# One hybrid decoder layer on one core: full-row attention scores, priority for partial-sum copies and additions, and a shifted first softmax

## The chip, the cores and the metric

The kernel runs on one core of a Trainium2 chip. The metric is device time in microseconds (us). Its engines are named as in the profile: PE multiplies matrices (PEld loads its stationary operand), DVE, ACT and POOL work on vectors, SP starts most DMAs. PE's granted clock is given as a share of full speed: 1.00 is the 2.4 GHz level, 0.50 the 1.2 GHz level.

## The reference

One layer for 512 tokens of 1024 features, in float32. After an RMS norm one wide projection gives the inputs of two branches. Branch A is causal attention in a window of 128 tokens with 8 query heads and 2 key heads of 64 features, a relative-position bias from a table, and a learned sink per head that joins the softmax's maximum and denominator. Branch B is gated linear attention. Gates merge both; a SwiGLU feed-forward layer of 2816, a per-layer embedding gate and a final norm follow. What the change touches is this part:

```python
s = jnp.einsum('bnqhgd,bnkhd->bnhgqk', qb, kb) * (HEAD_DIM ** -0.5)
s = s + band_relative_bias(rel_table)
s = jnp.where(valid[None, :, None, None], s, -1e30)
m = jnp.maximum(jnp.max(s, axis=-1, keepdims=True), sink)
pr = jnp.exp(s - m)
denom = jnp.sum(pr, axis=-1, keepdims=True) + jnp.exp(sink - m)
o = jnp.einsum('bnhgqk,bnkhd->bnqhgd', pr / denom, vb)
```

## The kernel before

**Products.** Each float32 operand is split into a high part (a cast on ACT, L111) and a low part (a subtraction, L112, on DVE and in some cases on POOL). A product is then three matmuls, high by high, high by low and low by high (L121 to L123), added up in PSUM. Large projections go through a scheme of seven products in place of eight: `quad_pair` for one pair of output tiles, in four steps named for example qa0.0 to qa0.3. It keeps running sums in PSUM; between steps ACT copies an intermediate sum out of the bank in which PE continues (L542, L548, L554, L562; the tiles named u and v), and DVE adds (L534). The second step of a pair writes into the bank that the first copy reads, so PE waits for that copy. The sums of weight blocks that the scheme needs are made on POOL (L255); `Weights` loads, sums and splits the blocks a few units ahead of their use.

**Order.** Each engine works through a queue in a fixed order. A scheduler sets it from the order in which the program issues its instructions; work inside `tc.high_priority(offset=...)` is placed as though issued that much sooner. `drive(stream, other)` takes one step of a projection and then one step of another generator, so a `yield` decides beside which step a piece stands.

**Stages.** First come the norm and projection v0 with values and low-rank gates, then v2, then a small matmul that expands the bias table (bias_ps, from the copy rts), the attention keys (kaps), and v1, the rest of the linear branch's values (about 59 to 82 us). Then the attention queries qa0 and qa1 run (about 82 to 107 us), while the generator `log_decay` issues 16 scans (L705) that accumulate the linear branch's decay. Next are the linear branch's keys and queries, qk0 to qk3, and gates og0 and og1 (to about 226 us); `attention` is driven beside these.

**Attention.** There are 8 items, one for each block of 128 tokens and key head. Item j has the steps scores, transposes and values, and in between a softmax: bias added (L756), the maximum mx (L761), m with the sink (L764), its negative nm (L766), dl (L768), exponentials on ACT (L770, L773), de and rd (L775, L777) and scaling (L779). Transposes (L789) follow on PE. In items 0 and 1, the first block, scores are plain float32 matmuls of 64 rows (L750). In the others a score is two matmuls: L753 over 128 rows, in which the stationary tile holds the query's high and low parts in two halves and the moving tile the key's high part twice, and L754 over 64 rows, the query's high part by the key's low part. The low parts of the two key heads lie in one tile, kl, one in each half of its partitions.

Of the kernel before, what the change touches and what calls it, by code (L numbers as in the profile page):

```python
# [9 lines left out]
F32 = mybir.dt.float32  # L10
F32R = mybir.dt.float32r
# [22 lines left out]
def hybrid_layer(  # L34
# [427 lines left out]
                W.split_to(W.pos + u - 1)  # L462
        v0_evac(t, ps)

    hT.sums()


    bgk = cpool.tile([P, 4], F32, name="bgk")
    glag = cpool.tile([P, 2], F32, name="glag")
    sink = cpool.tile([P, 8], F32, name="sink")  # L470
    rt = cpool.tile([32, 8], F32, name="rt")
    oh = t2("oh")
    band = t2("band")
# [9 lines left out]
    nc.sync.dma_start(gple, norm_ple.rearrange("(k p o) -> p k o", p=P, o=1))  # L483
    nc.sync.dma_start(glag, gla_norm.rearrange("(j d) -> d j", d=P))
    nc.sync.dma_start(mraw, c_masks)
    nc.vector.tensor_scalar_mul(glag, glag, 0.5)
    masks = cpool.tile([P, 6, 32], U8, name="masks")
    nc.vector.tensor_copy(masks, mraw)


    def tok_inner(name, lhs, k0, nk, ncol, evac, per=2):
# [31 lines left out]
    def quad_pair(name, act, c, evac):  # L523

        pa, pb, pc = (bank(f"{name}p{x}") for x in "abc")
        H = (slice(0, 256), slice(256, 512))

        def product(ps, w, i, x, first=True):
            hi, lo = act.q(x)
            for k in range(4):  # L530
                mm3(ps, (w[0][:, i, k, :], w[1][:, i, k, :]), (hi[:, k, :], lo[:, k, :]), first and k == 0, k == 3, not first)

        def add(out, a, b):
            nc.vector.tensor_tensor(out=out, in0=a, in1=b, op=ALU.add)  # L534


        part = t2(f"{name}u"), t2(f"{name}v")
        p1, u2, u3, u4 = (part[i // 2][:, H[i % 2]] for i in range(4))
        run = pa[:, H[0]]
        w = W.take(f"{name}.0")  # L540
        product(run, w, 0, "b11")
        nc.scalar.copy(p1, run)  # L542
        product(pb[:, H[0]], w, 1, "b21")
        add(c[0][:, H[0]], pb[:, H[0]], p1)
        yield
        w = W.take(f"{name}.1")
        product(run, w, 1, "t2", False)
        nc.scalar.copy(u2, run)  # L548
        product(pc[:, H[0]], w, 0, "t1")
        add(u4, pc[:, H[0]], u2)  # L550
        yield
        w = W.take(f"{name}.2")
        product(run, w, 1, "t3", False)
        nc.scalar.copy(u3, run)  # L554
        product(pb[:, H[1]], w, 0, "b22")
        add(c[0][:, H[1]], pb[:, H[1]], u4)
        evac(0)
        add(c[1][:, H[1]], pc[:, H[0]], u3)
        yield
        w = W.take(f"{name}.3")  # L560
        product(run, w, 0, "t4", False)
        nc.scalar.copy(c[1][:, H[0]], run)  # L562
        evac(1)
        yield

# [51 lines left out]


    ps = bank("bias_ps")
    rts = t2("rts", (32, 16, 8))  # L620
    nc.vector.tensor_copy(rts, rt.unsqueeze(1).broadcast_to([32, 16, 8]))
    nc.tensor.matmul(ps[:, 0:NB], lhsT=rts.rearrange("b r h -> b (r h)"), rhs=oh[0:32, 0:NB], start=True, stop=True)
    bv = t2("bv")
    nc.vector.tensor_tensor(out=bv[:, 0:NB], in0=ps[:, 0:NB], in1=band[:, 0:NB], op=ALU.add)
# [10 lines left out]
    qa = a8("qa")  # L635


    qs = []
    k3 = a8("k3", (P, 3, 512), F32R)
    ks, kl = [k3[:, g, :] for g in range(2)], k3[:, 2, :]  # L640
    half = (slice(0, 64), slice(64, 128))

    def stack_k():
        for g in range(2):
            split((ks[g][half[g]], kl[half[g]]), k_aT[half[g]], eng=nc.gpsimd)
            nc.sync.dma_start(ks[g][half[1 - g]].bitcast(F32), ks[g][half[g]].bitcast(F32))

    def stack_q(i):
# [81 lines left out]
    def attention():  # L730
# [8 lines left out]
        def scores(j):  # L739
# [4 lines left out]
            for pair in range(2):  # L744
                ps = bank(f"sc{j}{pair}").rearrange("p (a b) -> p a b", a=2)
                keys = slice(kb * P, (n + 1) * P)
                for a in range(2):
                    h = 2 * pair + a
                    if n == 0:
                        nc.tensor.matmul(ps[:, a, :w], lhsT=qa[rows, h, tok(n)], rhs=k_aT[rows, 0:P], start=True, stop=True)  # L750
                        continue
                    q = qs[g][:, h, tok(n)]
                    nc.tensor.matmul(ps[:, a, :w], lhsT=q, rhs=ks[g][:, keys], start=True, stop=False)  # L753
                    nc.tensor.matmul(ps[:, a, :w], lhsT=q[rows], rhs=kl[rows, keys], start=False, stop=True)  # L754
                hs = slice(g * 4 + 2 * pair, g * 4 + 2 * pair + 2)
                nc.vector.scalar_tensor_tensor(  # L756
                    out=s[:, 2 * pair : 2 * pair + 2, :], in0=ps[:, :, :w], scalar=0.125, in1=bias[:, hs, 256 - w : 256],
                    op0=ALU.mult, op1=ALU.add,
                )
            mx = sm.tile([P, 4], F32, tag="mx", name=f"mx{j}")  # L760
            nc.vector.reduce_max(mx, s, axis=AX.X)  # L761
            m = sm.tile([P, 4], F32, tag="m", name=f"m{j}")
            sk = sink[:, 4 * g : 4 * g + 4]
            nc.vector.tensor_tensor(out=m, in0=mx, in1=sk, op=ALU.max)  # L764
            nm = sm.tile([P, 4], F32, tag="nm", name=f"nm{j}")
            nc.vector.tensor_scalar_mul(nm, m, -1.0)  # L766
            dl = sm.tile([P, 4], F32, tag="dl", name=f"dl{j}")
            nc.vector.tensor_tensor(out=dl, in0=sk, in1=m, op=ALU.subtract)  # L768
            es = sm.tile([P, 4], F32, tag="es", name=f"es{j}")
            nc.scalar.activation(es, dl, AF.Exp)  # L770
            su = sm.tile([P, 4], F32, tag="su", name=f"su{j}")
# [33 lines left out]
            if g:  # L805
                split(oaT.part(0, ALL, tok(n)), pov[n].rearrange("p (t q) -> p t q", t=4))

        yield
        for j in range(len(items) + 1):
            if j < len(items):  # L810
                scores(j)
                yield
            if j:
                transposes(j - 1)
                yield
                values(j - 1)
                if j != 2:
                    yield
# [559 lines left out]
```

## Time and profile before

| | us |
|---|---|
| median of 3 runs (lowest to highest) | 904.01 (902.99 to 907.49) |
| profiled execution, its own time | 906.57 |
| its span | 904.6 |
| PE busy (share of span) | 866.4 (96%) |
| DVE busy | 607.8 (67%) |
| ACT busy | 462.9 (51%) |
| POOL busy | 282.2 (31%) |

The mean granted clock of PE is 0.989. Shares of busy time are means over stages: PE is nearly always at work, so what remains is where it is not, where it runs at the lower clock, and how long its own instructions take. In the rows below a line such as L753 is a line of the kernel before; "idle before <-" names what ended an engine's idle time.

### The profile page before, as it was taken

What the parts mean: (1) busy time and instruction counts of PE and PEld (TensorE: products, weight loads), DVE (VectorE), ACT (ScalarE), POOL (GpSimd) and SP (SyncE); (2) the same over time, 40 slices, a digit from 0 to 9 for tenths busy, and PEclk for the clock granted to TensorE, in tenths of its full rate; (3) what the DMA queues carried; (4) which work ended last, traced back from release to release, by engine and by line L of the source; (5) the groups of instructions that cost most, each with busy time, mean ns of one, the idle gap of its engine ahead of it and who ended that gap; (6) DMA issues with size and microseconds to landing.
All of it is one profiled execution on the core that took longest, in us unless ns stands there. A gap on an engine that the chain in (4) does not pass through costs nothing.

```text
span 904.6 us, 15452 instructions
## 1 busy us (share of the span) xinstructions
PE 866.4 (96%) x6062; PEld 761.4 (84%) x6062; DVE 607.8 (67%) x874; ACT 462.9 (51%) x915; POOL 282.2 (31%) x229
## 2 busy tenths in 40 slices
PE   7889879999999999999999999999999999999996
PEld 5878777778977778888888899988999889998886
DVE  5768965666978753435459799734899536985564
ACT  5346665667766543423227655522566314554453
POOL 3673773333021110010033356022565034530001
PEclk9999979999999999999999999999999999999999
DMA  8364431124463444695213433432233422244502
GB/s 251 95 153 125 151 92 49 47 71 151 136 210 120 156 141 153 221 353 202 94 49 116 141 93 94 152 105 69 75 113 96 141 93 71 94 138 132 174 1 94
DMA packets 88235, 113.33 MB, mean 125 GB/s; under 512 B 6145, under 2 KB 64289, under 8 KB 87778
## 3 DMA queue, kind: packets, MB, share of 16 engines
q1 hardware_dynamic: 86706, 107.43, 37.5%
q0 software_dynamic: 1456, 4.92, 1.9%
q8 instruction: 47, 0.77, 0.4%
q14 instruction: 26, 0.21, 0.1%
HBM read 95.35 MB, written 15.93 MB: 123 GB/s over the span
## 4 chain that ended last, share of the span: by engine, by line
PE 79%; DVE 11%; issue 4%; ACT 3%; POOL 1%; DMA 1%; SPq 0%; POOLq 0%; ACTq 0%; DVEq 0%
DVE u L1257 2%; PE pov L801 1%; PE lv L892 1%; PE yaps L121 1%; PE sc L754 1%; PE yaps L123 1%; PE gt0ps L121 1%; PE gt0ps L123 1%; PE wo0ps L123 1%; PE wo0ps L121 1%; PE gt0ps L122 1%; PE yaps L122 1%; PE fo10ps L121 1%; PE fo10ps L122 1%; PE fo00ps L122 1%
## 5 line engine op out<-in xcount | busy, mean ns | idle before, releaser
L342 POOL TENSOR_TENSOR or<-om,mhalf 128x1 f32<-128x1 f32 x16 | 12.3, 770 | 63.8 <-DVE om L346 63.8
L111 ACT CAST act_h<-u 128x512 fp32r<-128x512 f32 x22 | 13.7, 622 | 27.2 <-DVE u L1257 27.2
L1257 DVE TENSOR_TENSOR u<-u,g 128x512 f32<-128x512 f32 x22 | 25.6, 1164 | 0.4
L884 DVE TENSOR_TENSOR zs<-zs,kq 128x512 f32<-128x512 f32 x28 | 19.8, 724 | 5.8 <-ACT zs L880 5.8
L342 POOL TENSOR_TENSOR h20r<-h20n,mhalf 128x1 f32<-128x1 f32 x1 | 0.6, 562 | 72.1 <-DVE h20n L351 72.1
L756 DVE SCALAR_TENSOR_TENSOR s_all<-sc,bias 128x512 f32<-128x512 f32 (+1 forms) x16 | 9.9, 622 | 11.6 <-PE sc L754 11.2
L976 ACT ACTIVATE own<-o,or 128x256 f32<-128x256 f32 x16 | 7.6, 475 | 18.6 <-POOL or L342 18.5
L878 DVE TENSOR_TENSOR zs<-G 128x512 f32<-128x512 f32 x24 | 15.8, 684 | 0.1
L773 ACT ACTIVATE s_all<-s_all,nm 128x256 f32<-128x256 f32 (+1 forms) x32 | 14.9, 469 | 1.5 <-DVE nm L766 1.5
L112 DVE TENSOR_TENSOR act_l<-u,act_h 128x512 fp32r<-128x512 f32 x22 | 14.9, 680 | 0.0
L801 PE MATMUL pov<-pT,kv 128*64 128x512 f32 x28 | 14.4, 612 | 0.4 <-ACT pT L791 0.4
L779 ACT ACTIVATE s_all<-s_all,rd 128x256 f32<-128x256 f32 (+1 forms) x32 | 12.8, 472 | 3.2 <-DVE rd L777 3.1
L1254 ACT ACTIVATE g<-g 128x512 f32<-128x512 f32 x22 | 13.9, 630 | 0.3
L121 PE MATMUL yaps<-qs,pa_h 128*128 128x512 f32 x32 | 13.6, 425 | 0.0
L879 ACT ACTIVATE zs<-zs 128x256 f32<-128x256 f32 x28 | 11.7, 419 | 3.5 <-DVE zs L878 3.0
L789 PE MATMUL pt<-ident,s_all 128*128 128x128 f32 x56 | 9.0, 285 | 4.5 <-ACT s_all L779 4.5
L1147 POOL DMA_DIRECT2D xr<-in_x x4 | 2.2, 566 | 34.9 <-PE gg3pb L123 34.9
L111 ACT CAST mx_h<-yg 128x512 fp32r<-128x512 f32 x8 | 5.0, 622 | 15.5 <-DVE yg L1092 15.5
L121 PE MATMUL gt0ps<-gt_h,xT_h 128*128 128x512 f32 x32 | 12.8, 401 | 0.0
L1243 POOL TENSOR_TENSOR r<-x10m,mhalf 128x1 f32<-128x1 f32 x1 | 0.6, 562 | 39.2 <-DVE x10m L351 39.2
L121 PE MATMUL wo0ps<-wo_h,mx_h 128*128 128x512 f32 x32 | 12.6, 395 | 0.0
L121 PE MATMUL wo1ps<-wo_h,mx_h 128*128 128x512 f32 x32 | 12.6, 395 | 0.0
(2782 smaller groups left out, 3839.6 us busy)
## 6 DMA issues: line engine op xcount, KB each, us to landing
mg<-mgd SPq DMA_DIRECT2D x8, 512.0 KB, 6.6
vd<-v_g SPq DMA_DIRECT2D x2, 1024.0 KB, 5.2
sild<-gw SPq DMA_DIRECT2D x8, 256.0 KB, 2.1
own<-vd SPq DMA_DIRECT2D x4, 512.0 KB, 5.2
own<-sild SPq DMA_DIRECT2D x4, 512.0 KB, 5.0
mgd<-gw SPq DMA_DIRECT2D x8, 256.0 KB, 2.6
ogd<-og SPq DMA_DIRECT2D x8, 256.0 KB, 3.5
mgd<-sgg SPq DMA_DIRECT2D x8, 256.0 KB, 4.5
```

The costliest lines, as they stand in the source:

```text
L111: nc.scalar.copy(hi, src)
L112: eng.tensor_tensor(out=lo, in0=src, in1=hi.bitcast(F32), op=ALU.subtract)
L121: nc.tensor.matmul(ps, lhsT=l[0], rhs=r[0], start=first, stop=False, **kw)
L122: nc.tensor.matmul(ps, lhsT=l[0], rhs=r[1], start=False, stop=False, **kw)
L123: nc.tensor.matmul(ps, lhsT=l[1], rhs=r[0], start=False, stop=last, **kw)
L342: return r, nc.gpsimd.tensor_tensor(out=r, in0=a, in1=mhalf, op=ALU.pow)
L773: nc.scalar.activation(s[:, a, :], s[:, a, :], AF.Exp, bias=nm[:, a : a + 1], accum_out=su[:, a : a + 1])
L801: nc.tensor.matmul(pov[n][rows, :], lhsT=v_a[:, kb + b, rows], rhs=pTs[j][b], start=(b == 0), stop=(b == nk - 1))
L878: pe.tensor_tensor(out=z3, in0=g3, in1=g3[:, :, b - 1 : b].broadcast_to([P, nb, 2 * b]), op=ALU.subtract)
L884: nc.vector.tensor_tensor(out=d4, in0=d4, in1=kq_, op=ALU.mult)
L1254: nc.scalar.activation(gs[e], gs[e], AF.Silu)
L1257: nc.vector.tensor_tensor(out=us[e], in0=us[e], in1=gs[e], op=ALU.mult)
```

## The change

Five edits are made:

- Copies and additions of `quad_pair` are issued with high priority (offset 1000). This holds for all its uses, in the feed-forward layer too.
- The low parts of the keys get a tile for each key head, kl[0] and kl[1], in which the other half's 64 partitions are set to zero by a POOL memset; the second score matmul goes over all 128 rows.
- The maximum is taken negated, with min against a negated sink `nsink`, so that the multiplication by -1 for each item is gone.
- In `attention` the first empty step is taken out and put in behind the second item's scores: scores 0 and 1 are issued one step sooner, and transposes 0 stand beside the same step as before.
- The copy `rts` is issued with the other constants, ahead of v2; the sums of the normed input (`hT.sums()`) are issued behind the constants.

```diff
@@ -462,12 +462,11 @@
                 W.split_to(W.pos + u - 1)
         v0_evac(t, ps)
 
-    hT.sums()
-
 
     bgk = cpool.tile([P, 4], F32, name="bgk")
     glag = cpool.tile([P, 2], F32, name="glag")
     sink = cpool.tile([P, 8], F32, name="sink")
+    nsink = cpool.tile([P, 8], F32, name="nsink")
     rt = cpool.tile([32, 8], F32, name="rt")
     oh = t2("oh")
     band = t2("band")
@@ -483,9 +482,14 @@
     nc.sync.dma_start(gple, norm_ple.rearrange("(k p o) -> p k o", p=P, o=1))
     nc.sync.dma_start(glag, gla_norm.rearrange("(j d) -> d j", d=P))
     nc.sync.dma_start(mraw, c_masks)
+    rts = t2("rts", (32, 16, 8))
+    nc.vector.tensor_copy(rts, rt.unsqueeze(1).broadcast_to([32, 16, 8]))
     nc.vector.tensor_scalar_mul(glag, glag, 0.5)
+    nc.vector.tensor_scalar_mul(nsink, sink, -1.0)
     masks = cpool.tile([P, 6, 32], U8, name="masks")
     nc.vector.tensor_copy(masks, mraw)
+
+    hT.sums()
 
 
     def tok_inner(name, lhs, k0, nk, ncol, evac, per=2):
@@ -530,8 +534,14 @@
             for k in range(4):
                 mm3(ps, (w[0][:, i, k, :], w[1][:, i, k, :]), (hi[:, k, :], lo[:, k, :]), first and k == 0, k == 3, not first)
 
+
         def add(out, a, b):
-            nc.vector.tensor_tensor(out=out, in0=a, in1=b, op=ALU.add)
+            with tc.high_priority(offset=1000):
+                nc.vector.tensor_tensor(out=out, in0=a, in1=b, op=ALU.add)
+
+        def copy(out, a):
+            with tc.high_priority(offset=1000):
+                nc.scalar.copy(out, a)
 
 
         part = t2(f"{name}u"), t2(f"{name}v")
@@ -539,19 +549,19 @@
         run = pa[:, H[0]]
         w = W.take(f"{name}.0")
         product(run, w, 0, "b11")
-        nc.scalar.copy(p1, run)
+        copy(p1, run)
         product(pb[:, H[0]], w, 1, "b21")
         add(c[0][:, H[0]], pb[:, H[0]], p1)
         yield
         w = W.take(f"{name}.1")
         product(run, w, 1, "t2", False)
-        nc.scalar.copy(u2, run)
+        copy(u2, run)
         product(pc[:, H[0]], w, 0, "t1")
         add(u4, pc[:, H[0]], u2)
         yield
         w = W.take(f"{name}.2")
         product(run, w, 1, "t3", False)
-        nc.scalar.copy(u3, run)
+        copy(u3, run)
         product(pb[:, H[1]], w, 0, "b22")
         add(c[0][:, H[1]], pb[:, H[1]], u4)
         evac(0)
@@ -559,7 +569,7 @@
         yield
         w = W.take(f"{name}.3")
         product(run, w, 0, "t4", False)
-        nc.scalar.copy(c[1][:, H[0]], run)
+        copy(c[1][:, H[0]], run)
         evac(1)
         yield
 
@@ -617,8 +627,6 @@
 
 
     ps = bank("bias_ps")
-    rts = t2("rts", (32, 16, 8))
-    nc.vector.tensor_copy(rts, rt.unsqueeze(1).broadcast_to([32, 16, 8]))
     nc.tensor.matmul(ps[:, 0:NB], lhsT=rts.rearrange("b r h -> b (r h)"), rhs=oh[0:32, 0:NB], start=True, stop=True)
     bv = t2("bv")
     nc.vector.tensor_tensor(out=bv[:, 0:NB], in0=ps[:, 0:NB], in1=band[:, 0:NB], op=ALU.add)
@@ -635,14 +643,17 @@
     qa = a8("qa")
 
 
+
     qs = []
-    k3 = a8("k3", (P, 3, 512), F32R)
-    ks, kl = [k3[:, g, :] for g in range(2)], k3[:, 2, :]
+    k4 = a8("k4", (P, 4, 512), F32R)
+    ks, kl = [k4[:, g, :] for g in range(2)], [k4[:, 2 + g, :] for g in range(2)]
     half = (slice(0, 64), slice(64, 128))
+    for g in range(2):
+        nc.gpsimd.memset(kl[g][half[1 - g]].bitcast(F32), 0.0)
 
     def stack_k():
         for g in range(2):
-            split((ks[g][half[g]], kl[half[g]]), k_aT[half[g]], eng=nc.gpsimd)
+            split((ks[g][half[g]], kl[g][half[g]]), k_aT[half[g]], eng=nc.gpsimd)
             nc.sync.dma_start(ks[g][half[1 - g]].bitcast(F32), ks[g][half[g]].bitcast(F32))
 
     def stack_q(i):
@@ -751,21 +762,19 @@
                         continue
                     q = qs[g][:, h, tok(n)]
                     nc.tensor.matmul(ps[:, a, :w], lhsT=q, rhs=ks[g][:, keys], start=True, stop=False)
-                    nc.tensor.matmul(ps[:, a, :w], lhsT=q[rows], rhs=kl[rows, keys], start=False, stop=True)
+                    nc.tensor.matmul(ps[:, a, :w], lhsT=q, rhs=kl[g][:, keys], start=False, stop=True)
                 hs = slice(g * 4 + 2 * pair, g * 4 + 2 * pair + 2)
                 nc.vector.scalar_tensor_tensor(
                     out=s[:, 2 * pair : 2 * pair + 2, :], in0=ps[:, :, :w], scalar=0.125, in1=bias[:, hs, 256 - w : 256],
                     op0=ALU.mult, op1=ALU.add,
                 )
             mx = sm.tile([P, 4], F32, tag="mx", name=f"mx{j}")
-            nc.vector.reduce_max(mx, s, axis=AX.X)
-            m = sm.tile([P, 4], F32, tag="m", name=f"m{j}")
+            nc.vector.tensor_reduce(out=mx, in_=s, axis=AX.X, op=ALU.max, negate=True)
             sk = sink[:, 4 * g : 4 * g + 4]
-            nc.vector.tensor_tensor(out=m, in0=mx, in1=sk, op=ALU.max)
             nm = sm.tile([P, 4], F32, tag="nm", name=f"nm{j}")
-            nc.vector.tensor_scalar_mul(nm, m, -1.0)
+            nc.vector.tensor_tensor(out=nm, in0=mx, in1=nsink[:, 4 * g : 4 * g + 4], op=ALU.min)
             dl = sm.tile([P, 4], F32, tag="dl", name=f"dl{j}")
-            nc.vector.tensor_tensor(out=dl, in0=sk, in1=m, op=ALU.subtract)
+            nc.vector.tensor_tensor(out=dl, in0=sk, in1=nm, op=ALU.add)
             es = sm.tile([P, 4], F32, tag="es", name=f"es{j}")
             nc.scalar.activation(es, dl, AF.Exp)
             su = sm.tile([P, 4], F32, tag="su", name=f"su{j}")
@@ -805,10 +814,12 @@
             if g:
                 split(oaT.part(0, ALL, tok(n)), pov[n].rearrange("p (t q) -> p t q", t=4))
 
-        yield
         for j in range(len(items) + 1):
             if j < len(items):
                 scores(j)
+                yield
+            if j == 1:
+
                 yield
             if j:
                 transposes(j - 1)
```

From about 226 us on, the order is the same on all five engines. Ahead of that it moves. The first place is ACT's queue between the end of the query projection qa1 and the start of qk1; qs are the queries' high parts, qk0u and qk0v the intermediate sums of qk0 that are copied from PSUM. Before:

```order
L562 COPY qa<-qa1pa 128x256
L111 CAST qs_1035<-qa 64x2x384
L111 CAST qs_1036<-qa 64x2x384
L542 COPY qk0u<-qk0pa 128x256
L111 CAST qk1.0_h<-qk1r_981 128x512
L111 CAST qk1.0_h<-qk1r_1122 128x512
L548 COPY qk0u<-qk0pa 128x256
L111 CAST qk1.1_h<-qk1.0s_1157 128x1024
```

ACT's queue at the same place with the change:

```order
L544 COPY qa<-qa1pa 128x256
L111 CAST qs_1039<-qa 64x2x384
L544 COPY qk0u<-qk0pa 128x256
L111 CAST qs_1040<-qa 64x2x384
L111 CAST qk1.0_h<-qk1r_985 128x512
L111 CAST qk1.0_h<-qk1r_1126 128x512
L544 COPY qk0u<-qk0pa 128x256
L782 ACT_TABLE_LOAD
```

The first copy of qk0u stands between the two casts of qs, where it stood behind both.

The second place is DVE's queue while qa1 runs; G are the scans (SCALAR_TENSOR_TENSOR here, TENSOR_TENSOR_SCAN in the trace), names that end in _l are weights' low parts, qa with three names on L534 or L540 are additions. Before:

```order
L112 TENSOR_TENSOR qa1.0_l<-qa1r_762,qa1.0_h 128x512
L112 TENSOR_TENSOR qa1.1_l<-qa1.0s_851,qa1.1_h 128x1024
L534 TENSOR_TENSOR qa<-qa0pb,qa0v 128x256
L534 TENSOR_TENSOR qa<-qa0pc,qa0v 128x256
L705 SCALAR_TENSOR_TENSOR G<-G,E 128x128 x2
L112 TENSOR_TENSOR qa1.2_l<-qa1.0s_852,qa1.2_h 128x1024
L112 TENSOR_TENSOR qa1.3_l<-qa1r_762,qa1.3_h 128x512
L112 TENSOR_TENSOR qa<-qa,qs_1035 64x2x384
L534 TENSOR_TENSOR qa<-qa1pb,qa1u 128x256
```

DVE's queue at the same place with the change:

```order
L112 TENSOR_TENSOR qa1.0_l<-qa1r_766,qa1.0_h 128x512
L540 TENSOR_TENSOR qa<-qa0pb,qa0v 128x256
L716 SCALAR_TENSOR_TENSOR G<-G,E 128x128 x4
L112 TENSOR_TENSOR qa1.1_l<-qa1.0s_855,qa1.1_h 128x1024
L716 SCALAR_TENSOR_TENSOR G<-G,E 128x128 x4
L112 TENSOR_TENSOR qa<-qa,qs_1039 64x2x384
L540 TENSOR_TENSOR qa<-qa1pb,qa1u 128x256
L112 TENSOR_TENSOR qa1.2_l<-qa1.0s_856,qa1.2_h 128x1024
L716 SCALAR_TENSOR_TENSOR G<-G,E 128x128
L112 TENSOR_TENSOR qa1.3_l<-qa1r_766,qa1.3_h 128x512
```

Before, two scans stand between qa1.1_l and qa1.2_l and one more ahead of this piece; with the change eight stand ahead of qa1.2_l, and the low part of the queries' first half as well.

The third place is DVE's queue at the first softmax; sc are the scores' PSUM banks, mx, m, nm and dl the steps named above, kq and qk0v sums of qk0. Before:

```order
L756 SCALAR_TENSOR_TENSOR s_all<-sc_1261,bias 128x2x128
L756 SCALAR_TENSOR_TENSOR s_all<-sc_1265,bias 128x2x128
L112 TENSOR_TENSOR qk1.1_l<-qk1.0s_1157,qk1.1_h 128x1024
L761 TENSOR_REDUCE mx_1269<-s_all 128x4
L534 TENSOR_TENSOR kq_1193<-qk0pc,qk0v 128x256
L764 TENSOR_TENSOR m_1271<-mx_1269,sink 128x4
L766 TENSOR_SCALAR nm_1273<-m_1271 128x4
L768 TENSOR_TENSOR dl_1275<-sink,m_1271 128x4
L534 TENSOR_TENSOR kq_1193<-qk0pb,qk0v 128x256
L756 SCALAR_TENSOR_TENSOR s_all<-sc_1329,bias 128x2x128
L756 SCALAR_TENSOR_TENSOR s_all<-sc_1333,bias 128x2x128
L112 TENSOR_TENSOR qk1.2_l<-qk1.0s_1158,qk1.2_h 128x1024
```

DVE's queue at the same place with the change, from the first maximum on:

```order
L772 TENSOR_REDUCE mx_1243<-s_all 128x4
L775 TENSOR_TENSOR nm_1245<-mx_1243,nsink 128x4
L777 TENSOR_TENSOR dl_1247<-sink,nm_1245 128x4
L540 TENSOR_TENSOR qk0v<-qk0pc,qk0u 128x256
L767 SCALAR_TENSOR_TENSOR s_all<-sc_1294,bias 128x2x128
L767 SCALAR_TENSOR_TENSOR s_all<-sc_1298,bias 128x2x128
L772 TENSOR_REDUCE mx_1302<-s_all 128x4
L784 TENSOR_TENSOR de_1256<-su_1251,es_1249 128x4
L775 TENSOR_TENSOR nm_1304<-mx_1302,nsink 128x4
L786 RECIPROCAL rd_1258<-de_1256 128x4
L777 TENSOR_TENSOR dl_1306<-sink,nm_1304 128x4
L112 TENSOR_TENSOR qk1.1_l<-qk1.0s_1161,qk1.1_h 128x1024
```

With the change the first item's mx, nm and dl stand together and the second item's follow behind qk0v; qk1.1_l, which stood within the first chain, stands behind both, and qk1.2_l five rows further on.

## Rows read from the trace of the kernel before

**Rows 1.** Stretches: PE, PEld, DVE, ACT, POOL busy (instructions), granted clock, DMA share, GB/s.

```profile
34.00:59.00 25.00, 20.07 (x125) 17.69 (x124) 19.90 (x21) 9.29 (x17) 13.77 (x14) 0.93 0.44 137
59.00:82.00 23.00, 23.00 (x180) 21.66 (x179) 16.93 (x18) 14.02 (x24) 13.56 (x14) 1.00 0.72 148
82.00:114.00 32.00, 25.70 (x198) 23.95 (x196) 31.82 (x41) 23.82 (x36) 19.43 (x11) 1.00 0.44 144
114.00:135.00 21.00, 16.64 (x98) 15.84 (x99) 13.58 (x24) 12.52 (x37) 17.17 (x12) 0.76 0.30 81
135.00:226.00 91.00, 90.03 (x579) 71.55 (x578) 55.60 (x98) 58.57 (x148) 32.93 (x25) 1.00 0.28 82
```

**Rows 2.** PE's waits: what waited, for what, us in total, times, longest.

```profile
PE pt L789 <- ACT s_all L779: 4.5, 2, 4.0
PE qk0pa L121 <- ACT qk0u L542: 4.1, 1, 4.1
PE bias_ps L622 <- issue: 2.3, 1, 2.3
PE qa1pa L121 <- ACT qa1u L542: 1.5, 1, 1.5
```

**Rows 3.** The stretches at half clock, columns as in rows 1.

```profile
52.30:55.60 3.30, 3.30 (x10) 2.52 (x9) 1.60 (x3) 0.00 (x0) 3.28 (x5) 0.50 0.23 52
113.70:120.50 6.80, 6.10 (x27) 5.88 (x28) 2.90 (x4) 2.87 (x6) 6.72 (x5) 0.50 0.12 18
130.80:134.10 3.30, 3.07 (x15) 3.07 (x16) 1.11 (x4) 3.27 (x15) 1.91 (x2) 0.50 0.08 8
```

**Rows 4.** PE, timeline around one score group: start us, duration us, instruction.

```profile
139.75 0.28 PE L123 MATMUL qk1pc<-h_t,qk1.1_l 128*128 128x256 f32 x1
139.87 0.28 PE L753 MATMUL sc<-k,qs 128*128 128x256 f32 x1
140.08 0.38 PE L754 MATMUL sc<-k,qs 64*128 64x256 f32 x1
140.39 0.39 PE L753 MATMUL sc<-k,qs 128*128 128x256 f32 x1
...
142.27 0.38 PE L121 MATMUL qk1pa<-h_t,qk1.2_h 128*128 128x256 f32 x1
```

**Rows 5.** PE's instructions by line, 135 to 226 us: busy us, mean ns.

```profile
L753 PE MATMUL sc<-k,qs 128*128 128x256 f32 x24 | 8.8, 368 | 0.0
```

**Rows 6.** Weight loads of the same score group, timeline.

```profile
139.75 0.19 PEld L753 LDWEIGHTS sc<-k,qs 128*128 128x128 f32 x1
...
140.39 0.19 PEld L753 LDWEIGHTS sc<-k,qs 128*128 128x128 f32 x1
```

**Rows 7.** DVE, timeline, the bias table's copy.

```profile
50.47 0.21 DVE L621 COPY rts<-rt 32x128 f32<-32x128 f32 x1
```

**Rows 8.** DVE, timeline, low parts for v1.

```profile
66.50 3.48 DVE L112 TENSOR_TENSOR v12.1_l<-v12.0s,v12.1_h 128x512 fp32r<-128x512 f32 x2
```

**Rows 9.** ACT and DVE around the q projections: timeline, then scans by line.

```profile
112.26 1.68 ACT L111 CAST qs<-qa 64x768 fp32r<-64x768 f32 x2 [4.03 <-DVE qa L534]
103.95 1.22 DVE L705 TENSOR_TENSOR_SCAN G<-G,E 128x128 f32<-128x128 f32 x1
L705 DVE TENSOR_TENSOR_SCAN G<-G,E 128x128 f32<-128x128 f32 x16 | 9.5, 633 | 0.2 <-ACT E L701 0.2
```

**Rows 10.** The stretch of the q projections, columns as in rows 1.

```profile
80.30:116.20 35.90, 29.20 (x218) 27.27 (x217) 35.56 (x45) 26.98 (x39) 21.55 (x12) 0.97 0.39 129
```

**Rows 11.** DVE, timeline, within the first softmax.

```profile
121.67 2.35 DVE L112 TENSOR_TENSOR qk1.1_l<-qk1.0s,qk1.1_h 128x1024 fp32r<-128x1024 f32 x1
125.22 1.21 DVE L766 TENSOR_SCALAR nm<-m 128x4 f32<-128x4 f32 x1
127.41 1.43 DVE L112 TENSOR_TENSOR qk1.2_l<-qk1.0s,qk1.2_h 128x1024 fp32r<-128x1024 f32 x1
```

**Rows 12.** POOL's memsets of line 866: duration ns min/median/max, first and last start.

```profile
L866 POOL MEMSET sc<- x4: 525/526/527, 222.6 to 295.7; 128x512 f32 x4
```

## The prediction, made before the changed kernel was run

> **What bounds the kernel now.** I read four views in this order: the stretches, PE's waits, the single rows around the places they name, and the order in which each engine receives its instructions before and after.
>
> The stretches come first [rows 1]. The order of instructions is the same on all five engines from about 226 us on, so a first-hand effect can only lie ahead of that; there the table shows where PE, the engine with the most work, is not working. In 59 to 82 it is busy all of 23.00 us, in 135 to 226 it is busy 90.03 of 91. The holes are in 34 to 59 (20.07 of 25.00), 82 to 114 (25.70 of 32.00: 6.3 us lost) and 114 to 135 (16.64 of 21.00: 4.4 lost). The waits say what ends them [rows 2]: the transposes of the first softmax wait 4.0 us for ACT's scaling, the second step of the first key/query projection 4.1 for a copy, the bias matmul 2.3, the second step of the last attention-query projection 1.5. Third, three stretches run at a granted clock of 0.50, the 1.2 GHz level, each around one of these holes [rows 3]: PE is busy 3.30, 6.10 and 3.07 us there, so at 1.00 the same work would take half, and they cost 1.65, 3.05 and 1.54 us.
>
> So two kinds of saving are possible: PE work that gets shorter (135 to 226, where PE never waits), and holes that close (34 to 135). An edit that only relieves DVE or ACT after 135 gives nothing.
>
> **Scores with 128 rows.** Six of the eight items have two key blocks; each issues eight matmuls, a 128-row one (L753) and a 64-row one (L754) in turn, 24 of each in all [rows 5]. The timeline shows what that costs [rows 4]: of the group that starts at 139.87, the second starts 0.21 later, the third 0.31 after that, and the next product starts at 142.27, 2.40 us after the first. Six groups are 14.4 us. The projection's matmul just ahead has the same 128 rows and 256 columns and is followed 0.12 later (139.75 to 139.87). With 128 rows everywhere, 48 matmuls at 0.12 are 5.8 us: **-8.6**. What makes the difference can be seen in the weight loads [rows 6]: the load for the score at 139.87 begins at 139.75, beside the matmul before; the load for the score at 140.39 begins only at 140.39, with its own matmul, after the 64-row one has been let through. Bounds: 0 (the pace of 0.30 stays) to -8.6 with nothing more to win; I take the end at 0.12, because 0.12 is the pace of every other full-row product of these columns.
> Against it stands a rule of the Trainium skill, TensorE: Matmul & The Clock Gate, Part 3, section The mechanism: a weight load overlaps running matmuls only when it goes to other rows of the array. By it, full-row loads one after another would not overlap, and a score would take a load of 0.19 and then its own 0.12, as much as now: -0. The first row of rows 6 disagrees: that load has the same 128 rows as the matmul beside which it runs. The rule stays as rival 3.
> Behind the pair matmuls the softmaxes now get their scores some 1.4 us sooner, and PE reaches the transposes sooner by the same amount. Since PE waits in 135 to 226 for 1.0 us in all, I charge 0 for that, with 1 us as the bound.
>
> **The bias table's copy.** The copy of rt on DVE runs at 50.47 [rows 7], behind h's last split, and the bias matmul has waited 2.28 us for it, right ahead of the attention-key projection, on whose matmuls the half clock then lies (52.3 to 55.6). In the changed order it is issued with the constants, some twenty DVE instructions earlier; its input is an early load. The wait goes (-2.3), and with it likely the low clock (-1.65): -3.9. But a part is handed back: v1, behind the key projection, takes low parts that DVE makes one after another while POOL works, each pair some 3.5 us [rows 8], and these don't come sooner by the whole amount. I take 1.4 back, **-2.5**; bounds 0 (DVE's splits take it all) to -3.9.
>
> **Copies and additions first; the first softmax a step earlier.** In 82 to 135 five things change.
> (a) Before the second step of qk0, ACT does both casts of qs (1.68 for two [rows 9]) and then the copy that PE waits for; the casts themselves wait 4.03 us for an addition on DVE, which stands behind six scans. In the new order the copy stands between the two casts (0.84 sooner), and three of the scans come after the addition (3 x 0.63 = 1.9, mean of the sixteen [rows 9]). Of the 4.1 us wait, 2.7 goes; the rest stays. I count **-2.5**.
> (b) Before the second step of qa1 the copy also stands behind one cast rather than two: 0.84 of the 1.5 us wait, **-0.7**.
> (c) The first softmax. Its scores move from behind step two of qk0 to ahead of it, and its transposes stay where they were. The two splits qk1.1_l (2.35) and qk1.2_l (1.43), which stood within its chain on DVE, go behind it, and the nm instruction (1.21) is gone [rows 11]. Those 5 us alone exceed the 4.0 us wait of the transposes, which I take down to 0.3: **-3.7**.
> (d) The low clock at 113.7 and 130.8 follows the holes in (a) and (c). I count about 60% of 3.05 + 1.54 as regained: **-2.8**.
> (e) Against these, scans that stood late now stand ahead of two weight splits: eight rather than three come before qa1.2_l. DVE is already 35.56 of 35.90 us busy from 80.3 to 116.2 [rows 10], so what is moved ahead delays what is behind it: five scans at 0.63 are 3.2, of which some cover is there: **+2.0**.
> Sum **-7.7**. All holes and low clocks of the stretch are 10.7 + 4.6 = 15.3; bounds 0 to -15.
>
> **The rest.** Eight nm instructions fewer on DVE and the negated reduction: beyond (c), DVE is 55.60 of 91 busy in 135 to 226 and hides them, 0. The nsink multiplication stands among constants, ahead of an instruction that waits for a load anyway. Two memsets of 64 partitions on POOL: a 128-partition one takes 525 ns [rows 12], so about 1 us at most in front of the key split, while POOL works 13.56 of 23 us there: 0, or 1 if the last weight sum of v1 is met. Two activation table loads fewer on ACT: ACT is not what is waited for there, 0. On SP three loads are requested behind one or two others; no PE wait of this stretch is for a load, 0 with +1.5 as the bound.
>
> **Sum:** -8.6 - 2.5 - 7.7 = -18.8. The profiled execution took 906.57 us (span 904.6), so 887.8 by that; its own time is 2.6 above the median of 904.01, from which the same sum gives **885**.
>
> **The rivals.**
> 1. DVE keeps what the q projections gain. For it: 35.56 of 35.90 busy, and every scan, split and addition of before still has to pass there ahead of the same products. Against: nm and two splits leave the chain that ends the stretch. Then only the scores and the bias count: 904.0 - 8.6 - 2.5 = 893. Chance 0.22.
> 2. All holes and low clocks of 34 to 135 named here close: 904.0 - 8.6 - 3.9 - 15.3 = 876. For it: the same four waits account for nearly all of them. Against: (e). Chance 0.10.
> 3. Full rows bring nothing, the 0.30 stays: 904.0 - 2.5 - 7.7 = 894. For it: the scores change their weights with every matmul, and their two kinds now use the same rows. Against: so do the projection's matmuls, at 0.12 [rows 4, 6]. Chance 0.04.
> 4. Slower: priority sends the scans ahead of qa1.1_l and qa1.2_l while POOL is making weight sums. A scan beside POOL's work took 1.22 us [rows 9], against 0.63 in the mean; if all sixteen take 1.22, DVE has 16 x 0.59 = 9.4 more, PE waits for low parts twice more, and two more low-clock stretches like that at 113.7 cost 6.1: 15.5 in place of -7.7. 904.0 - 11.1 + 15.5 = 908.4. It decides from the point where the stretch 82 to 135 gets longer by more than 11.1 us, what scores and bias give. The SBUF page of the Trainium skill (SBUF — State Buffer, Who interferes with whom) says that DVE and GpSimd share a port pair under an exclusive lock; the 1.22 us scan agrees, the others show that it is not the usual case. Chance 0.04.
>
> **The numbers.** 0.60 for the forecast (880 to 890). Range 875 to 897: it takes in rivals 1 to 3 and leaves out mainly what lies between rival 1 and no change, and rival 4. What a measurement can tell from no change is 0.5%, 4.5 us: faster means under 899.5. Forecast and rivals 1 to 3 are there, 0.96; some of that I give to an unforeseen stall, so faster 0.94, within 0.5% 0.03, slower 0.03.
>
> **What would show it.** Scores: groups of eight in about 1.0 us rather than 2.40, each weight load beginning ahead of its own matmul. Bias: no wait of the bias matmul, clock 1.00 on the key projection; v1 then shows new waits of about 1.4 us for low parts. Stretch to the first transposes: copy of qk0 behind one cast, PE's wait for it about 1.5, for the first transposes under 0.5, and a new wait of about 2 for qa1.2_l. From the start of the sliding-window values at about 136 to 226 us the stage is shorter by the 8.6 alone; from there all stages last as before. The prediction is wrong if the score groups stay above 2 us, or if first transposes come no sooner against the end of v1 than before.

## The result, and the profile after

The changed kernel takes 894.61 us (median of 4 runs, 893.57 to 895.27) where the kernel before takes 904.42: a ratio of 0.9882, with a 95% interval of 0.9856 to 0.9908. A second measurement gave 893.18 us and 0.9869 (0.9850 to 0.9888). The forecast was 885, a gain of 19 us; the gain is 10 to 12. The profiled execution took 895.27 us with a span of 893.1, 11.5 less than before's 904.6.

To see where these 11.5 are, I cut both traces at the same instructions of PE: the first matmul of v2, of v1, of qa0, of the second step of qk1, of the linear branch's levels, of the feed-forward layer, and of the next tensor there, fu00. Columns are as in [rows 1]; the second number is the length of the stage. Before:

```profile
33.92:58.79 24.87, 19.94 (x123) 17.49 (x123) 19.98 (x21) 9.19 (x16) 13.82 (x14) 0.93 0.43 133
58.79:82.47 23.68, 23.68 (x182) 21.97 (x180) 17.40 (x19) 14.58 (x25) 13.59 (x15) 1.00 0.71 148
82.47:137.24 54.77, 44.11 (x305) 40.98 (x305) 46.01 (x66) 37.54 (x74) 36.70 (x23) 0.91 0.39 121
137.24:226.44 89.20, 88.23 (x571) 70.56 (x569) 54.95 (x97) 57.34 (x146) 32.83 (x25) 1.00 0.27 80
226.44:494.00 267.56, 267.56 (x2061) 220.41 (x2061) 164.65 (x255) 129.04 (x265) 35.41 (x41) 1.00 0.50 165
494.00:507.10 13.10, 10.76 (x74) 10.08 (x73) 10.01 (x15) 7.43 (x14) 3.47 (x3) 0.87 0.46 147
```

The same stages after the change:

```profile
33.20:55.67 22.47, 19.82 (x124) 17.87 (x123) 20.14 (x20) 9.18 (x16) 11.38 (x11) 0.92 0.36 107
55.67:78.97 23.30, 23.30 (x182) 21.99 (x180) 16.81 (x18) 11.15 (x21) 17.07 (x20) 1.00 0.84 189
78.97:129.36 50.39, 42.02 (x303) 39.41 (x302) 42.69 (x63) 36.67 (x76) 32.39 (x21) 0.93 0.37 121
129.36:212.88 83.52, 79.81 (x571) 68.02 (x570) 57.53 (x91) 58.16 (x147) 36.72 (x27) 1.00 0.30 92
212.88:480.43 267.55, 267.55 (x2061) 220.38 (x2061) 164.57 (x255) 129.00 (x265) 35.50 (x41) 1.00 0.49 165
480.43:495.25 14.82, 11.58 (x73) 11.11 (x72) 10.05 (x15) 7.43 (x14) 4.27 (x4) 0.77 0.45 143
```

| stage | forecast | lengths after less before |
|---|---|---|
| v2, bias, key projection, v1 (first two rows) | -2.5 | -2.4 - 0.4 = -2.8 |
| qa0 to qk1's first step, with the first softmax (third row) | -7.7 | -4.4 |
| other softmaxes, six score groups (fourth row) | -8.6 | -5.7 |
| linear branch's levels (fifth row) | 0 | 0.0 |
| start of the feed-forward layer (sixth row) | 0 | +1.7 |

The remaining -0.4 (-0.7 ahead of v2 and +0.3 behind the table) lies where the change does nothing. In the fourth stage PE was busy 88.23 of 89.20 us and is now busy 79.81 of 83.52: its work fell by 8.4, but its idle time rose from 1.0 to 3.7. In the last row the order of the work is the same; the granted clock is 0.77 in place of 0.87. In the trace of the second measurement ("the change again" below) the stages are the same within 0.1 us but for the first: v2 to the key projection takes 20.96 us at a clock of 1.00, where it takes 22.47 at 0.92 here.

The scores behave as forecast. Two views of one group after the change, PE and the weight loads, with the product behind it at 133.29:

```profile
132.33 0.28 PE L764 MATMUL sc<-k,qs 128*128 128x256 f32 x1
132.45 0.28 PE L765 MATMUL sc<-k,qs 128*128 128x256 f32 x1
132.57 0.28 PE L764 MATMUL sc<-k,qs 128*128 128x256 f32 x1
...
133.29 0.28 PE L121 MATMUL qk1pa<-h_t,qk1.2_h 128*128 128x256 f32 x1
```

```profile
132.22 0.19 PEld L764 LDWEIGHTS sc<-k,qs 128*128 128x128 f32 x1
132.34 0.19 PEld L765 LDWEIGHTS sc<-k,qs 128*128 128x128 f32 x1
```

Eight matmuls take 0.96 us where they took 2.40 [rows 4]; each load begins 0.11 ahead of its own matmul [rows 6 for before], beside the matmul in front.

The waits of PE, against [rows 2]:

```profile
PE qk0pa L121 <- ACT qk0v L544: 4.3, 1, 4.3
PE qa1pa L123 <- DVE qa1.2_l L112: 3.3, 1, 3.3
PE pov L810 <- ACT pT L800: 2.8, 2, 1.6
...
PE pt L798 <- ACT s_all L788: 0.9, 1, 0.9
PE qa1pa L121 <- ACT qa1u L544: 0.7, 1, 0.7
```

The waits for the bias copy, for qk0u (4.1) and most of that of the first transposes (4.0) are gone. In their place stand one for qk0v, one for qa1.2_l and one of the value matmuls.

### The profile page after: what moved, and what is told of

Read it like the earlier page. It is cut to its first block, busy times and chain, and to the rows that moved or that the text cites. A ratio compares the mean times of both kernels' runs of the same rounds, so it can differ in the third digit from the quotient of the medians.

```text
span 893.1 us, 15437 instructions
## 1 busy us (share of the span) xinstructions
PE 856.6 (96%) x6062; PEld 759.5 (85%) x6062; DVE 605.7 (68%) x867; ACT 459.1 (51%) x913; POOL 281.2 (31%) x231
## 4 chain that ended last, share of the span: by engine, by line
PE 79%; DVE 11%; issue 4%; ACT 3%; DMA 1%; POOL 1%; SPq 0%; POOLq 0%; ACTq 0%; DVEq 0%
DVE u L1268 2%; PE pov L810 1%; DVE G L716 1%; PE lv L903 1%; PE yaps L121 1%; PE yaps L123 1%; PE gt0ps L123 1%; PE gt0ps L122 1%; PE wo0ps L121 1%; PE wo0ps L123 1%; PE yaps L122 1%; PE fo10ps L122 1%; PE fo00ps L122 1%; PE gt0ps L121 1%; PE fo11ps L123 1%
## 5 line engine op out<-in xcount | busy, mean ns | idle before, releaser
L716 DVE TENSOR_TENSOR_SCAN G<-G,E 128x128 f32<-128x128 f32 x16 | 13.8, 903 | 0.5 <-ACT E L712 0.5
L121 PE MATMUL v0ps<-v_h,h_h 128*128 128x400 f32 x32 | 12.0, 376 | 1.0 <-ACT h_h L111 1.0
L121 PE MATMUL gt0ps<-gt_h,xT_h 128*128 128x512 f32 x32 | 12.8, 400 | 0.0
```

Of the source, the lines that this page charges most:

```text
L121: nc.tensor.matmul(ps, lhsT=l[0], rhs=r[0], start=first, stop=False, **kw)
L716: nc.vector.tensor_tensor_scan(out=G[:, h, tok(c)], data0=G[:, h, tok(c)], data1=E[:, h, tok(c)], initial=0.0, op0=ALU.add, op1=ALU.add,)
```

## The experiments

Theories: A, the gains of the q projections and the first softmax were eaten by single new waits that come with the order of instructions, first of all by scans ahead of qa1.2_l; B, DVE, ACT and the softmax chain are full there, and an edit of the order only decides which product waits. Each expectation says what A and B give in its case. Each ratio is to the kernel before, run on the same chip, with its 95% interval.

**Scores alone, memsets on POOL.** The kernel before with

```diff
-    ks, kl = [k3[:, g, :] for g in range(2)], k3[:, 2, :]
+    ks, kl = [k4[:, g, :] for g in range(2)], [k4[:, 2 + g, :] for g in range(2)]
+    for g in range(2): nc.gpsimd.memset(kl[g][half[1 - g]].bitcast(F32), 0.0)
-    nc.tensor.matmul(ps[:, a, :w], lhsT=q[rows], rhs=kl[rows, keys], ...)
+    nc.tensor.matmul(ps[:, a, :w], lhsT=q, rhs=kl[g][:, keys], ...)
```

> The kernel before with full-row scores alone (zeroed key tiles for each head, memsets on POOL as in the change). Theory A: the six score groups fall from 2.40 to about 1.0 us (-8.6), softmax chains take 2 to 3 of it back, and the memsets on POOL lead the scheduler to put scans ahead of the weight split qa1.2_l, which makes PE wait and costs about 5: net -1, about 903 (900 to 905), with a PE wait for qa1.2_l of 3 us or more. Theory B (scans in another order cost nothing): -6, about 898. Theory C (full rows are kept in full): -8.6, about 895.5.

897.11 us, 0.9916 (0.9896 to 0.9936): 7.6 us by the ratio. The memsets on POOL alone bring the late scans ahead of qa1.2_l, without any priority; but PE's longest wait is now 4.5 us for an addition on DVE, the wait for qk0u is 0.2 where it was 4.1, and the way from v1's first matmul to the second step of qk1 is not longer for it (77.1 us, 78.5 before).

**Scores alone, memsets on DVE.**

```diff
-        nc.gpsimd.memset(kl[g][half[1 - g]].bitcast(F32), 0.0)
+        nc.vector.memset(kl[g][half[1 - g]].bitcast(F32), 0.0)
```

> As the run before, but the two memsets on DVE instead of POOL; the order of scans and weight splits is then as in the kernel before. Theory A: the wait for qa1.2_l is gone, what remains is the scores less what the softmax takes, -6, about 898.5, and about 5 us faster than with the memsets on POOL. Theory B: the same time as with the memsets on POOL. Theory C: 895.5.

896.34 us, 0.9911 (0.9893 to 0.9929). With the old order of scans it is as fast as with the new one: theory A's 5 us do not exist. By their gains, 7.6 and 8.0, both runs lie nearest to theory C, though the interval of the first (5.8 to 9.4) takes in theory B's 6 too. The traces decide it: the fourth stage lasts 81.0 us in both, 8.2 less than before, and the value matmuls wait 0.4 as before. Without the other edits nearly all of the 8.6 is kept.

**The whole change, memsets on DVE** (the same edit in the changed kernel).

> The whole change, with the two memsets on DVE instead of POOL: three scans ahead of qa1.2_l instead of eight. Theory A: PE's wait of 3.3 us for qa1.2_l and the low clock behind it go, 894.6 - 4.5 = 890 (888 to 892). Theory B (DVE is full there whatever the order): 894.6, the wait only moves to a later product.

893.89 us, 0.9878 (0.9859 to 0.9897), as the change itself. The wait for qa1.2_l is gone, but waits of 2.0 for qk0u and 4.0 of the value matmuls have come. The three scans of the expectation are a miscount: in this trace, as in the kernel before, ten scans run ahead of qa1.2_l, and eight of them ahead of qa1.0_l.

**Bias copy alone.** The copy rts moved among the constants, nothing else.

> The kernel before with the bias table's copy issued among the constants, and nothing else. Theory A: the wait of 2.3 us goes and the low clock leaves the key projection, v1 gives little back: -2.8, about 901.5. Rival: DVE's low parts for v1 or for the q projections take it all back, 904 within 1.

903.51 us, 0.9985 (0.9973 to 0.9996): 1.4 us, between the two. In its trace the first two rows of the table come out as the prediction had them: v2 to the key projection 3.9 shorter, at a clock of 1.00, and v1 1.9 longer.

**The change without priority.** `copy` and `add` of quad_pair without `tc.high_priority`.

> The whole change without the priority of copies and additions. Theory A (the copies that come behind one cast instead of two are worth what the prediction counted): PE's waits for qa1u and qk0u come back, 894.6 + 2 = about 896.5. Theory B (DVE and ACT are full there and in the softmax; priority only decides who waits): within 1 of 894.6, with fewer waits of the value matmuls for pT (under 1 us instead of 2.8).

891.31 us, 0.9865 (0.9845 to 0.9885). Not slower than the change, against theory A; but theory B's "under 1 us" failed too: the value matmuls still wait 2.5.

**The change without the step shift.**

```diff
+        yield
         for j in range(len(items) + 1):
...
-            if j == 1:
-                yield
```

> The whole change without the step shift of the first scores (the empty first step is back; the negated maximum stays). Theory A (the shift takes away the 4.0 us wait of the first transposes): that wait is back, 894.6 + 3.5 = 898. Theory B: 895 to 896, since the shift trades that wait for the one of 4.3 us for the copy qk0v, which stands behind exponentials on ACT.

893.25 us, 0.9885 (0.9868 to 0.9901), the same time. The transposes wait 3.6 again, and the wait of 4.3 for qk0v is gone: the shift exchanges one for the other.

**pT copies first.** The change with the memsets on DVE, and

```diff
+                with tc.high_priority(offset=1000):
-                nc.scalar.copy(pT, pst)
+                    nc.scalar.copy(pT, pst)
```

and the same around de, rd and the scaling.

> The change with the memsets on DVE, and with the pT copies, the denominators and the scaling of the softmax issued with the same priority as the sums. Theory A (in 135 to 226 us the value matmuls wait because ACT has exponentials ahead of the pT copies): the waits of the value matmuls, 4.0 us in the version with the memsets on DVE, fall under 1 us, 893.9 - 2.5 = 891.4. Rival (the softmax is late whatever the order): waits move to the transposes, 893.9 within 1.

889.45 us, 0.9845 (0.9823 to 0.9866). Faster than forecast, although one wait of the value matmuls, 2.2, stays.

**Scores and bias copy, nothing else.**

> The kernel before with full-row scores (memsets on POOL) and the early bias copy, and neither priority, shift nor negated maximum. Theory A (those three are worth 5 us and more): 900. Theory B (they give about 1 in all): 895.5, the sum of the two runs of one edit each (897.1 - 1.9).

892.79 us, 0.9878 (0.9863 to 0.9893). Two of the five edits give the whole gain. The fourth stage takes 81.1 us here, and the value matmuls wait 0.4.

**The change again,** beside the next three.

> The change itself once more, to be compared on one chip with the three runs beside it. All theories: a ratio to the kernel before of 0.988, about 894.

893.18 us, 0.9869 (0.9850 to 0.9888).

**Without 12 scans.**

```diff
-            for c in range(NT):
+            for c in range(NT if h == 0 else 0):
```

> The change without 12 of the 16 scans of the decay on DVE (three of four heads of the linear branch then run on sums that were not accumulated; the work behind is the same). Theory A (DVE's amount of work sets when qk0's second step can start, whatever the order): PE's wait of 3.3 us for qa1.2_l goes and does not come back elsewhere, qk0's second step starts 4 to 6 us earlier against the start of v1, and 889 to 890. Rival (the waits come from the order of ACT and the softmax chain): 893 to 894, the time lost again before the first transposes.

887.34 us, 0.9806 (0.9789 to 0.9823), 5.8 below the change beside it. From v1's first matmul to the second step of qk0 it is 52.0 us, 2.7 less than with the change (54.7) and not the 4 to 6 of theory A: PE's wait for qa1.2_l fell from 3.3 to 0.5, and one of 1.3 for a low part on POOL came. In the traces of all versions with every scan, whose waits are in different places, this distance is 53.7 to 57.5 (55.6 before), so versions with the same work differ by up to 3.8. The scans take 14.5 us of DVE with the change and 1.6 here. So 12.8 us less work on DVE brought 2.7: the amount of this work has a part in the distance, but that it sets the distance whatever the order is not shown. More of the gain lies behind it: against the trace of the change beside it, the way to the second step of qk1 is 1.9 shorter (the wait for qk0v is 2.3 in place of 4.4) and the start of the feed-forward layer 2.0 shorter, at a clock of 1.00, while v2 is 1.5 longer, at a lower clock.

**pT copies first, no priority for the sums.** Memsets on DVE, shift and negated maximum as in the change.

> Scores, bias copy, step shift and negated maximum of the change, memsets on DVE, priority for the pT copies, denominators and scaling, but none for the sums. Theory A (priority of the sums costs in the softmax stage): 888 or less, below the 889.5 of the same version with priority for the sums. Rival (it does not matter any more once the pT copies go first): 889.5 within 1.

889.01 us (888.86 to 889.45), 0.9825 (0.9808 to 0.9841): the fastest version with all of the work, 4.2 below the change on the same chip. The value matmuls no longer appear among its waits of 0.9 us or more.

**The same without any priority.**

> As the run before but without any priority. Theory A (the pT copies behind exponentials cost 2 to 3 us in 135 to 226 us): 891.5, with waits of the value matmuls of 2 us or more. Rival (those waits come with the priority of the sums): waits under 1 us and 889.

892.14 us (891.47 to 892.76), 0.9858 (0.9841 to 0.9876). The value matmuls wait 4.1 us in all:

```profile
PE pov L804 <- ACT pT L794: 4.1, 4, 1.9
PE qk0pa L121 <- ACT qk0u L547: 3.0, 1, 3.0
```

So this wait needs no priority of the sums. Putting the pT copies first, with the denominators and the scaling, is worth 3.1 us; the two runs' ranges don't touch, and in the traces it is the fourth stage that is shorter, 79.7 us in place of 83.3. What the pT copies are worth without the other two was not run. How much the priority of the sums itself costs stays open: 893.89 against 892.14 with the memsets on DVE, 894.61 against 891.31 on POOL, in each case from different chips and with intervals of the ratios that overlap. With the pT copies first it is 0.9845 against 0.9825. In all three pairs the version without this priority has the lower ratio, so no gain from it can be seen.

## Why the prediction was right, and where not

The direction, the range and PE's work in the largest single term were right; the sum of 18.8 was one and a half times to almost twice the gain, and the time lies outside 880 to 890, to which 0.60 was given. That it is the time of rivals 1 and 3 (893 and 894) is a coincidence: the pace of rival 3 is not there, and rival 1 has 8.6 for the scores and nothing for the third stage, where 5.7 and 4.4 were measured.

**Scores: right in PE's work and when made alone, wrong beside the other edits.** The 48 matmuls run at 0.12 us, and the rule of rival 3 does not hold here. "PE waits in 135 to 226 for 1.0 us in all, I charge 0 for that" held for the scores alone (fourth stage 8.2 shorter, value matmuls waiting 0.4). It failed for the five edits together (5.7 shorter, waiting 2.8): the other edits put exponentials ahead on ACT, and for that the prediction had no term. The chain in the changed kernel, ACT ahead of one value matmul:

```profile
169.15 0.50 ACT L782 ACTIVATE s_all<-s_all,nm 128x256 f32<-128x256 f32 x1
...
170.74 0.35 ACT L544 COPY kq<-qk3pa 128x256 f32<-128x256 f32 x1
170.99 0.51 ACT L782 ACTIVATE s_all<-s_all,nm 128x256 f32<-128x256 f32 x1
...
171.49 1.05 ACT L800 COPY pT<-pt 128x512 f32<-128x512 f32 x2
```

```profile
172.11 1.07 PE L810 MATMUL pov<-pT,kv 128*64 128x512 f32 x2 [1.59 <-ACT pT L800]
```

PE had finished the transposes and gone on to the next product at 168.85; the copies of their result stand in ACT's queue behind the next item's exponentials and start at 171.49. ACT at the same place in the version with scores and bias copy alone, where the copies are ahead:

```profile
172.27 1.06 ACT L794 COPY pT<-pt 128x512 f32<-128x512 f32 x2
...
173.33 0.51 ACT L776 ACTIVATE s_all<-s_all,nm 128x256 f32<-128x256 f32 x1
```

Issuing the copies, the denominators and the scaling first takes the wait from 4.1 to 0.3 and gives 3.1 us. The wait needs neither the priority (2.5 without it) nor the shift (2.8 without it). All versions with a wait of 2 us or more have the negated maximum, and of the versions without it none waits more than 0.4; no run has it alone, or the others without it, so which of the edits puts the exponentials ahead stays open.

**Bias copy: right as a sum**, 2.8 in the trace against 2.5, 1.4 in the timed run of this edit alone. Its parts came as forecast in the trace of that run (-3.9 and +1.9, forecast -3.9 and +1.4). In the change's they did not: the wait of 2.3 went, but a low clock fell in v2, and v1, which was to hand 1.4 back, is 0.4 shorter.

**(a), (b), (e): right as a sum, not singly.** The qk0u wait went entirely (4.1, forecast 2.5), qa1u fell from 1.5 to 0.7 as forecast, and (e) was mis-sized: 3.3 of wait for qa1.2_l in place of 2.0. It also rests on a wrong count. "Eight rather than three come before qa1.2_l" took only a piece of DVE's queue; the trace of the kernel before has ten scans ahead of it. Eight run from 83.25 to 89.7, ahead of qa1.0_l, and two more just in front; the rows with three of the eight and with these two:

```profile
85.09 1.05 DVE L705 TENSOR_TENSOR_SCAN G<-G,E 128x128 f32<-128x128 f32 x3
...
97.54 2.47 DVE L705 TENSOR_TENSOR_SCAN G<-G,E 128x128 f32<-128x128 f32 x2
99.94 1.19 DVE L112 TENSOR_TENSOR qa1.2_l<-qa1.0s,qa1.2_h 128x1024 fp32r<-128x1024 f32 x1
```

With the change no scan runs before 90.84, behind qa1.0_l, and eight come ahead of qa1.2_l, the last four of them here:

```profile
93.24 5.07 DVE L716 TENSOR_TENSOR_SCAN G<-G,E 128x128 f32<-128x128 f32 x4
98.23 0.92 DVE L112 TENSOR_TENSOR qa<-qa,qs 64x768 fp32r<-64x768 f32 x1
99.08 0.41 DVE L540 TENSOR_TENSOR qa<-qa1pb,qa1u 128x256 f32<-128x256 f32 x1
99.42 1.21 DVE L112 TENSOR_TENSOR qa1.2_l<-qa1.0s,qa1.2_h 128x1024 fp32r<-128x1024 f32 x1
100.55 0.41 DVE L716 TENSOR_TENSOR_SCAN G<-G,E 128x128 f32<-128x128 f32 x1
```

So the scans were not moved ahead, they came later, into the time in which POOL makes the sums of qk0's weights (93.46 to 96.1) and a low part of q (96.19 to 98.0). Of the four, the first, begun with POOL idle, takes 0.42 us, the other three 1.44, 1.45 and 1.99; the scan at 100.55, begun in POOL's pause, takes 0.41. The mean of the sixteen rose from 633 to 903 ns, 4.3 us in all. This is the price that rival 4 named, at a little under half of its 9.4; but it is the memsets on POOL that make the scans late and not, as rival 4 says, the priority: with the scores alone and the memsets on POOL the mean is already 812 ns, with the memsets on DVE it is 631 to 633 with priority or without. How the memsets do it stays open. In sum, the second step of qk0 came 0.9 us sooner against v1's start; the three terms had said 1.2. That little is gained here is what rival 1 says. Its reason, a full DVE, holds only in part: from qa0's first matmul to this step DVE is now busy 28.46 of 31.44 us, where it was 31.75 of 31.93.

**(c) failed.** "Those 5 us alone exceed the 4.0 us wait of the transposes, which I take down to 0.3" looked at one waiter. The transposes' wait went, but the exponentials that come sooner stand on ACT ahead of the copy of qk0v, for which PE's next step waits:

```profile
117.49 1.12 DVE L775 TENSOR_TENSOR nm<-mx,nsink 128x4 f32<-128x4 f32 x1
```

```profile
118.65 0.40 ACT L782 ACTIVATE s_all<-s_all,nm 128x128 f32<-128x128 f32 x1 [1.45 <-DVE nm L775]
...
121.23 0.40 ACT L782 ACTIVATE s_all<-s_all,nm 128x128 f32<-128x128 f32 x1
...
121.63 0.35 ACT L544 COPY qk0v<-qk0pa 128x256 f32<-128x256 f32 x1
```

```profile
122.03 0.58 PE L121 MATMUL qk0pa<-h_t,qk0.3_h 128*128 128x256 f32 x1 [4.33 <-ACT qk0v L544]
```

ACT was idle for 1.45 us while nm (a 128x4 instruction that takes 1.12 beside POOL) held back the exponentials, and the copy stood behind five of them and a cast of 1.03 us. Priority did not help: the copy stands there although it has priority. That the scheduler's own estimate had the exponentials ready first is likely, but was only argued. Without the shift the old wait of the transposes is back and the time is the same.

**(d) and the clock of the bias term failed.** I took 1.65 and 2.8 us as regained. In this execution the low clock moved instead:

```profile
36.00:40.00 4.00, 3.87 (x19) 3.87 (x20) 4.00 (x7) 1.96 (x5) 0.17 (x1) 0.57 0.66 197
100.00:106.00 6.00, 5.33 (x32) 5.33 (x33) 6.00 (x9) 1.34 (x2) 5.24 (x3) 0.72 0.59 161
120.00:126.00 6.00, 3.97 (x22) 3.97 (x23) 3.52 (x10) 5.42 (x20) 2.25 (x2) 0.72 0.69 204
486.00:494.00 8.00, 6.93 (x37) 6.64 (x37) 5.16 (x9) 4.83 (x10) 0.23 (x1) 0.57 0.74 231
```

Length times what is missing to 1.00 gives 1.7, 1.7, 1.7 and 3.4, 8.5 in all. Before, the three stretches of [rows 3] make 6.7 by the same measure and the start of the feed-forward layer shown above 1.7 (13.10 x 0.13), 8.4 in all. It left the key projection, and fell in v2, behind the new waits, and for longer in the feed-forward layer, whose work did not change. The mean granted clock of both profiled executions is 0.989. In the second profiled execution of the change v2 is at 1.00, so there the 1.65 of the bias term did come back, and 1.6 of the 8.4 in all; of (d), 1.7 came back in the third stage and was lost again in the feed-forward layer, in both executions.

**The memsets at 0 were right**: the two took 0.52 us each; their place in POOL's queue moved scans and splits, and that changed which product waits, not the time (897.11 against 896.34 with the scores alone, ratios of 0.9882 and 0.9878 with the whole change). Priority, shift and negated maximum together, -7.7 in the forecast, gave nothing that can be measured: 0.9878 without them, 0.9882 and 0.9869 with them.

## What to carry to other kernels

Where PE hardly waits, look at the copies that its next matmuls need and at what stands ahead of them in their engine's queue. Here a saving on PE came through almost whole when made alone, and by two thirds beside edits that changed that queue, until the copies were put first. When an edit moves work in a queue, count it over the whole trace and not over a piece of it, and look at what runs beside it in its new place. When several waits in a stretch follow one another, measure between two fixed points: here new orders removed waits of 4 us and moved the distance by at most 2. Time lost to a low clock should not be counted as regained because one hole closes; here 0 to 1.6 us of 4.5 came back.

## What was not expected of the hardware

A memset of 64 partitions by 512 took as long (0.52 us) as one of 128 partitions [rows 12].

DVE's smallest two-input instructions, nm, dl and de on 128x4 elements, come in two ranges of duration. In the changed kernel's softmaxes those that start while POOL is idle take 0.15 or 0.16 us, and the ten that start while POOL is at work take 0.47 to 1.27, until about the end of an instruction of POOL. Two rows of one item:

```profile
168.60 0.15 DVE L775 TENSOR_TENSOR nm<-mx,nsink 128x4 f32<-128x4 f32 x1
```

```profile
171.62 1.22 DVE L784 TENSOR_TENSOR de<-su,es 128x4 f32<-128x4 f32 x1
```

The number of inputs alone does not decide it. In the kernel before, one rd, a RECIPROCAL with one input, takes 0.18 at 130.31 with POOL at work throughout, but nm, there a TENSOR_SCALAR with one input, takes 1.10 to 1.23 the three times that it starts beside POOL (one is in [rows 11]) and 0.15 or 0.16 else. The Trainium skill, SBUF — State Buffer, section Who interferes with whom, gives DVE and GpSimd a shared port pair under an exclusive lock; these rows agree, and show that what counts is what POOL is doing, not how small the instruction is. In a chain of such instructions that matters more than one nm fewer.

The granted clock fell at the start of the feed-forward layer in several versions and not in others, with the same instructions there, and in v2 in one of two profiled executions of the same kernel; what decides it was not found.
